# Two-block fp32 model on one core: order and diagonals of the first product and its convolution rearranged, four modulation products moved behind it

## The chip, the cores and the metric

The kernel runs on one core of one Trainium2 chip. The metric is the device time of one execution in microseconds (us). TensorE (PE) multiplies, VectorE (DVE) and ScalarE (ACT) do elementwise work, GpSimd (POOL) a little of it, and SyncE (SP) issues nearly all transfers from memory, in one queue. Each engine takes its instructions in the order in which the program issues them; they wait for each other by semaphores.

## The reference, cut to what matters

Two model blocks on a sequence of 256 positions with 1024 features, all in fp32. The change touches only the beginning of the first one:

```
c_act = silu(c)
mod = c_act @ mod_w + mod_b                  # 6 vectors of 1024: sh_m, sc_m, gt_m, sh_f, sc_f, gt_f
h = rmsnorm(x, norm_pre_mix) * (1 + sc_m) + sh_m
u = h @ a_pw1_w + a_pw1_b                    # first product: 1024 -> 2048
a, gt = split(u)
u = a * sigmoid(gt)
u = causal_dwconv(u, a_dw_w) + a_dw_b        # depthwise, 31 taps
u = silu(layernorm(u, a_ln_g, a_ln_b))
y = u @ a_pw2_w + a_pw2_b                    # second product: 1024 -> 1024
x = x + gt_m * rmsnorm(y, norm_post_mix)
h = rmsnorm(x, norm_pre_ffn) * (1 + sc_f) + sh_f
...                                          # a feed-forward part, then the second block's two layers
```

## The kernel before

Activations lie with features on the partitions: eight input tiles of 128 features x 256 positions. A fp32 product is made of three passes of a rounded format: each operand is split into a high part (rounded) and a low part (what is left). For a weight block of 128 x 1024 (a unit), ScalarE makes the high part (`split_hi`, tile `whi`) and VectorE the low part (`split_lo`, tile `wlo`, the difference). Weights come two units (1 MB) at a time into three buffers `wraw`; a buffer is loaded again as soon as the second difference of its block is done.

The modulation `c_act @ mod_w` is not a TensorE product: for each of 48 groups of 128 outputs, a block `mraw` of 128 x 1024 is loaded (five buffers), VectorE multiplies it by the broadcast row `cact` (`mod_mult`), and ScalarE sums along the row (`mod_sum`). Groups 0 to 15 give shift and scale for the eight input tiles of the first product; 16 to 39 are needed behind the second product.

`pointwise_conv` begins with warm-up products on a zero tile, the broadcast of `cact`, and the root mean square of x (statistics tile `st`, square root, reciprocal, transposes into `bc`, copy `rms`). Then comes the first product, one input tile k after the other: VectorE makes two modulation products, ScalarE two sums, VectorE scales the tile (`scaled`), adds the bias to the two modulation values (`mod`), ScalarE modulates it (`y`) and rounds it (`xh`), VectorE makes the low part (`xl`), and TensorE makes 48 products (`pw1`) into eight banks of output tiles. The banks are turned into the convolution's inputs by a sigmoid on ScalarE (`sg`) and a product on VectorE (`up`); the sigmoid's bias lies in the table `vecs`, which `load_consts` loads.

The convolution of seven output tiles runs on TensorE: a diagonal tile (`conv_stack`, on GpSimd) holds the taps, and copies of the input shifted by 0 to 3 positions (`shifts`; TensorE, then `sh` by ScalarE) are multiplied by it. The eighth tile's 31 taps run on VectorE (`conv_dve`). A background list (`bg`) of small steps, taps and modulation products for groups 16 on, is worked off by `pump` between TensorE's parts: a call takes steps until their listed costs exceed its argument. A modulation step (`half` in `mod_later`) issues the sum of one group, the load of another and the product of the next. `pointwise_out` then ends the layer norm's statistics (`finish`), normalizes in five groups of tiles, and makes the second product (`gemm_square`): four input tiles into all outputs, then a tail in which TensorE's last output tiles alternate with VectorE's bias additions (`on_tiles`). `stream.split` inside these products keeps four units ahead.

Numbers that set the order: `MOD_LATE` modulation steps are left for the second product, `PUMPS` says after which of its input tiles they are issued and at what cost, `CV` how many roundings and differences of the second product's units are issued during the convolution and before the statistics, `LOS` in which groups of the normalization, `WARM_START` the numbers of warm-up products.

Of the kernel before, what the change touches and what calls it, by code (L numbers as in the profile page):

```python
# [25 lines left out]
MOD_LATE = 3  # L26
PUMPS = {3: 3}
CV = (5, 4)
LOS = (1, 2, 3)
MEMFILL = (4, 8, 2, 2)  # L30
WARM_START = (10, 6, 3, 24)
# [219 lines left out]
class Builder:  # L251
# [377 lines left out]
    def setup(self):  # L629
        nc = self.nc  # L630
        c = self.const
        first = "first" in self.parts
        x = self.xr.rearrange("p k t -> p (k t)")
        if first:
            self.cact = self.modp.tile([P, UNIT], F32, name="cact", bufs=1)
            nc.sync.dma_start(out=self.cact[0:1, :], in_=self.dr["c"])
        for h in range(2):
            c0 = slice(h * 4 * T, (h + 1) * 4 * T)
            nc.sync.dma_start(out=x[:, c0], in_=self.dr["x"][:, c0])
        self.head = c.tile([P, HEAD + P], F32, name="head")  # L640
# [3 lines left out]
        if first:  # L644
            self.taps = self.modp.tile([P, 288], F32, name="taps", bufs=1)
        else:
            self.load_consts()
        self.inv = c.tile([P, 1], F32, name="inv")
        nc.vector.memset(self.inv, 1.0 / 1024)
        self.one1 = c.tile([P, 1], F32, name="one1")  # L650
        nc.vector.memset(self.one1, 1.0)
        self.dummy = c.tile([P, 1], F32, name="dummy")
        self.preload(AF.Silu if first else AF.Sqrt)
        self.epst = {}
        for e in (RMS_EPS, LN_EPS, 4 * LN_EPS):
            self.epst[e] = c.tile([P, 1], F32, name=f"eps{len(self.epst)}")
            nc.vector.memset(self.epst[e], e)
        if self.need_mem:
            self.memk = c.tile([P, 2, T], F32, name="memk")
            self.memv = c.tile([P, 2, T], F32, name="memv")  # L660
# [240 lines left out]
    def conv_stack(self, cp, j):  # L901
# [4 lines left out]
        self.nc.gpsimd.tensor_tensor(out=t, in0=eye.unsqueeze(1).to_broadcast([P, 32, 32]),  # L906
# [8 lines left out]
    def pointwise_conv(self, cp):  # L915
# [3 lines left out]
        warm = self.xl[:, 0, :]  # L919
# [22 lines left out]
        def add(i, j, n):  # L942
            nc.vector.tensor_tensor(out=sq[:, i:i + n, :], in0=sq[:, i:i + n, :], in1=sq[:, j:j + n, :],
                                    op=ALU.add)

        for h, ps in enumerate(rows):
            nc.vector.tensor_copy(out=self.cact[:, 512 * h:512 * h + 512], in_=ps)
            add(4 * h, 4 * h + 2, 2)
            add(4 * h, 4 * h + 1, 1)
        add(0, 4, 1)  # L950
        st, bc = (self.ps_st.tile([P, 2, T], F32, name=nm, tag=nm) for nm in ("st", "bc"))
        for h in range(2):
            nc.tensor.matmul(st[:, 0, h:h + 1], lhsT=sq[:, 0, h * P:h * P + P], rhs=self.inv, start=True,
                             stop=True, skip_group_check=True)
        keep_warm(WARM_START[2])
# [4 lines left out]
        def mult(k):  # L960
            mods[k] = [self.mod_raw.pop(0) for _ in range(2)]
            for r in mods[k]:
                self.mod_mult(r)
                yield

        def sums(k):
            for h, r in enumerate(mods.pop(k)):
                self.mod_sum(r, h * KD + k)
                yield
            if self.n_mod < 2 * KD:  # L970
                self.mod_load(2)

        mult0, sums0 = mult(0), sums(0)
        next(mult0)
# [4 lines left out]
        keep_warm(WARM_START[3])  # L979
        rms = cp.tile([P, T], F32, name="rms", tag="sg", bufs=2)  # L980
        next(sums0)
        nc.scalar.copy(out=rms, in_=bc[:, 0, :])
        next(mult0)
# [6 lines left out]
        list(sums0)  # L990
# [6 lines left out]
        order = CONV_ORDER  # L997
        npe, ndv = N_PE_CONV, KD - N_PE_CONV
        first = [j for j in order if j >= ndv]
# [20 lines left out]
        for k in range(KD):  # L1020
            y, sh, sc = self.ys[:, k, 0, :], mod[:, 0, k:k + 1], mod[:, 1, k:k + 1]
            xh, xl = self.xh[:, k, :], self.xl[:, k, :]
            if k:
                next(mults)
                self.stream.split_hi()
                self.stream.split_hi()
                list(sums(k))
                self.stream.split_lo()
# [3 lines left out]
            if k:  # L1032
                nc.scalar.activation(out=y, in_=y, func=AF.Identity, scale=sc, bias=sh)
                nc.scalar.copy(out=xh, in_=y)
            else:
# [4 lines left out]
                self.stream.split_lo()  # L1040
            if k < KD - 1:
                mults = mult(k + 1)
                if k:
                    next(mults)
            nc.vector.tensor_tensor(out=xl, in0=y, in1=xh.bitcast(F32), op=ALU.subtract)
            if k == 0:
                next(mults)
# [74 lines left out]
        for n, j in enumerate(first):  # L1122
# [10 lines left out]
            if n >= npe - CV[0]:  # L1133
# [14 lines left out]
    def pointwise_out(self, st, later):  # L1148
# [3 lines left out]
        for _ in range(CV[1]):  # L1152
            self.stream.split_lo()
        bc = st.finish(LN_EPS, AF.Silu, False)
        groups = self.apply_tiles()
# [8 lines left out]
        for i, (k0, k1) in enumerate(groups):  # L1164
# [1129 lines left out]
```

## Time and profile before

| | us |
|---|---|
| three runs | 1480.75, 1483.52, 1484.99 (median 1483.52) |
| the profiled execution, device time | 1481.87 |
| its span, from first to last instruction | 1480.1 |
| TensorE busy in the span | 1419.9 (96%) |
| VectorE busy | 1076.0 (73%) |
| ScalarE busy | 853.8 (58%) |
| first product's matrix products, first to last | 16.9 to 73.0 |
| first tap of the convolution on VectorE | 74.0 |
| second product, first to last | 128.8 to 155 |
| first product of the feed-forward part | 180.3 |

All rows below are of the profiled execution, times from its span's start. A busy share of an engine counts an instruction that has begun and waits inside for another engine's access as busy. Durations of neighbours overlap a little, so that two instructions of 1.22 in a row take 2.35.

### The profile page before, as it was taken

The numbers are of one execution on the slowest core, as the hardware profiler recorded it, in microseconds if no ns is written. First come the engines' busy times: TensorE is split into PE (matmuls) and PEld (weight loads), VectorE is DVE, ScalarE is ACT, GpSimd is POOL, SyncE is SP. The second block draws the span as 40 slices with busy tenths as digits, with TensorE's granted clock in tenths as the row PEclk, the third lists the DMA queues.
The fourth block names the chain that finished last, engine by engine and source line by source line (L and its number), as shares of the span: only waits on it lengthen the run. The fifth ranks groups of instructions, "written<-read, shape, count | busy, mean of one in ns | idle before, by whom it ended". The sixth has DMA issues, their size and how long they took to land. (4 is left out here: it accounts for less than half of the span.)

```text
span 1480.1 us, 26075 instructions
## 1 busy us (share of the span) xinstructions
PE 1419.9 (96%) x10664; PEld 1273.4 (86%) x10664; DVE 1076.0 (73%) x1705; ACT 853.8 (58%) x1505; POOL 119.6 (8%) x113
## 2 busy tenths in 40 slices
PE   8888899999999999999999999999999999999997
PEld 7867799998888888898788888888888888888886
DVE  7897788885777656788568776678766765787754
ACT  6787566684655535751346555466554676565542
POOL 1210100001000010031010000110001111100011
PEclk9998899999999999999999999999999999999998
DMA  9774445565355553240024555536554342265540
GB/s 379 292 243 186 170 155 189 198 234 207 136 202 179 196 199 136 86 143 4 2 109 167 184 196 181 189 143 221 182 195 187 136 143 86 91 226 196 196 174 29
DMA packets 39145, 250.38 MB, mean 169 GB/s; under 512 B 4337, under 2 KB 4849, under 8 KB 12274
## 3 DMA queue, kind: packets, MB, share of 16 engines
q1 hardware_dynamic: 38594, 247.60, 45.9%
q8 instruction: 84, 1.38, 0.4%
q10 hardware_dynamic: 432, 1.11, 0.2%
q14 instruction: 35, 0.29, 0.1%
HBM read 247.65 MB, written 1.05 MB: 168 GB/s over the span
## 5 line engine op out<-in xcount | busy, mean ns | idle before, releaser
L235 DVE TENSOR_TENSOR wlo<-wraw,whi 128x1024 fp32r<-128x1024 f32 x416 | 514.3, 1250 | 34.1 <-ACT whi L226 33.4
L226 ACT CAST whi<-wraw 128x1024 fp32r<-128x1024 f32 x416 | 426.3, 1045 | 22.0 <-PE acc L378 5.6
L384 PE MATMUL acc<-hx,whi 128*128 128x512 f32 x880 | 310.7, 398 | 0.0
L384 PE MATMUL acc<-xx,whi 128*128 128x512 f32 x816 | 284.1, 390 | 0.0
L372 PE MATMUL acc<-xx,wlo 128*128 128x256 f32 x1008 | 280.7, 284 | 0.0
L372 PE MATMUL gu<-xx,wlo 128*128 128x256 f32 x1008 | 279.0, 282 | 1.6 <-ACT xx L625 1.0
L372 PE MATMUL acc<-hx,wlo 128*128 128x256 f32 x880 | 247.5, 281 | 0.0
L384 PEld LDWEIGHTS acc<-hx,whi 128*128 128x128 f32 x880 | 165.3, 188 | 40.5
L372 PEld LDWEIGHTS gu<-xx,wlo 128*128 128x128 f32 x1008 | 189.9, 189 | 4.9 <-ACT xx L625 1.7
L372 PEld LDWEIGHTS acc<-xx,wlo 128*128 128x128 f32 x1008 | 190.9, 191 | 0.8
L384 PEld LDWEIGHTS acc<-xx,whi 128*128 128x128 f32 x816 | 153.2, 188 | 32.1
L372 PEld LDWEIGHTS acc<-hx,wlo 128*128 128x128 f32 x880 | 166.1, 189 | 0.0
L384 PE MATMUL gu<-xx,whi 128*128 128x512 f32 x432 | 150.9, 390 | 0.0
L377 PE MATMUL gu<-xx,whi 128*128 128x256 f32 x512 | 148.4, 290 | 2.4 <-ACT u L894 2.4
L378 PE MATMUL gu<-xx,whi 128*128 128x256 f32 x512 | 142.9, 279 | 0.0
L1331 ACT ACTIVATE ys<-ys 128x256 f32<-128x256 f32 (+1 forms) x66 | 28.6, 437 | 151.7 <-DVE ys L1249 134.9
L377 PEld LDWEIGHTS gu<-xx,whi 128*128 128x128 f32 x512 | 96.2, 188 | 10.8 <-issue 7.9
L378 PEld LDWEIGHTS gu<-xx,whi 128*128 128x128 f32 x512 | 96.3, 188 | 0.7 <-issue 0.7
L384 PEld LDWEIGHTS gu<-xx,whi 128*128 128x128 f32 x432 | 81.1, 188 | 17.0
L1348 POOL TENSOR_TENSOR nsum<-ys 128x512 f32<-128x512 f32 (+1 forms) x9 | 12.4, 1380 | 871.1 <-PE acc L384 452.3
L858 ACT COPY lows<-acc 128x256 f32<-128x256 f32 x55 | 20.6, 374 | 97.8 <-PE acc L384 97.6
L1247 DVE SCALAR_TENSOR_TENSOR ys<-xr,acc 128x256 f32<-128x256 f32 x32 | 13.5, 422 | 75.0 <-PE acc L384 75.0
(397 smaller groups left out, 2351.5 us busy)
## 6 DMA issues: line engine op xcount, KB each, us to landing
wraw<-in_w SPq DMA_DIRECT2D x208, 1024.0 KB, 4.8
mraw<-in_mod SPq DMA_DIRECT2D x48, 512.0 KB, 5.5
xr<-in_x SPq DMA_DIRECT2D x2, 512.0 KB, 4.2
m<-in_mem SPq DMA_DIRECT2D x1, 1024.0 KB, 8.2
out<-xr SPq DMA_DIRECT2D x3, 256.0 KB, 2.2
cst<-in_consts SPq DMA_DIRECT2D x1, 546.0 KB
lora<-in_lora ACTq DMA_DIRECT2D x1, 384.0 KB, 3.4
lora_g<-in_lora ACTq DMA_DIRECT2D x1, 384.0 KB, 3.9
```

Source lines behind the costliest of these rows:

```text
L226: b.nc.scalar.copy(out=hi, in_=raw)
L235: b.nc.vector.tensor_tensor(out=lo, in0=raw, in1=hi.bitcast(F32), op=ALU.subtract)
L372: self.nc.tensor.matmul(out, lhsT=wl, rhs=x[:, 0, :], start=start, stop=False, skip_group_check=True)
L377: mm(out, lhsT=wh, rhs=x[:, 0, :], start=start, stop=False, skip_group_check=True)
L378: mm(out, lhsT=wh, rhs=x[:, 1, :], start=False, stop=False, skip_group_check=True)
L384: self.nc.tensor.matmul(bank, lhsT=wh, rhs=x, start=False, stop=stop, skip_group_check=True)
L858: nc.scalar.copy(out=lows[:, 1, :], in_=banks[1][:, 1, :])
L1247: self.nc.vector.scalar_tensor_tensor(out=y, in0=self.xr[:, k, :], scalar=2 * ALPHA, in1=ps[:, 1, :], op0=ALU.mult, op1=ALU.add)
L1331: b.nc.scalar.activation(out=b.ys[:, k0:k1, 1, :], in_=y, func=AF.Square)
L1348: e.tensor_tensor(out=out[:, q:2, :], in0=prev[:, q:2, :], in1=t[:, q:2, :], op=ALU.add)
```

## The change

- The table of taps is loaded as the second transfer of all, and five diagonals are made at the beginning, three of them on VectorE and two on GpSimd. Before, it was loaded behind input tile 1 and GpSimd made all five behind tile 2. The last two diagonals stay on GpSimd in the convolution.
- The squares of x are no longer added on VectorE; TensorE sums them with sixteen products of one column. The warm-up products go from 10, 6, 3, 24 to 10, 0, 14, on a tile that input tile 7 uses last.
- The operand of an input tile has its own function, called behind the product of the tile before. Both modulation products of a tile are made at its beginning, and the second rounding copy of its weights stands behind both sums.
- `load_consts` is called behind tile 6's product instead of tile 5's.
- In the convolution's background list a modulation product follows every second tap, where one followed every tap. Seven modulation steps instead of three are left for later: one is issued before the layer norm's statistics, one, two and two behind input tiles 1, 2 and 3 of the second product, the last one behind its tail.
- Before the statistics one difference is issued instead of four, one more behind them, and then one in each of four groups instead of three.

```
-MOD_LATE = 3
-PUMPS = {3: 3}
-CV = (5, 4)
-LOS = (1, 2, 3)
+MOD_LATE = 7
+PUMPS = {1: 1.1, 2: 2.2, 3: 2.2}
+CV = 5
...
-WARM_START = (10, 6, 3, 24)
+WARM_START = (10, 0, 14)
...
             nc.sync.dma_start(out=self.cact[0:1, :], in_=self.dr["c"])
+            self.taps = self.modp.tile([P, 288], F32, name="taps", bufs=1)
+            nc.sync.dma_start(out=self.taps, in_=self.dr["taps"])
...
-        warm = self.xl[:, 0, :]
+        warm = self.xl[:, KD - 1, :]
...
+        stacks = [self.conv_stack(cp, j, nc.vector if n < 3 else None)
+                  for n, j in enumerate(first[:N_STACK])]
         for h, ps in enumerate(rows):
             nc.vector.tensor_copy(out=self.cact[:, 512 * h:512 * h + 512], in_=ps)
-            add(4 * h, 4 * h + 2, 2)
-            add(4 * h, 4 * h + 1, 1)
-        add(0, 4, 1)
...
-        for h in range(2):
-            nc.tensor.matmul(st[:, 0, h:h + 1], lhsT=sq[:, 0, h * P:h * P + P], rhs=self.inv, start=True,
-                             stop=True, skip_group_check=True)
-        keep_warm(WARM_START[2])
+        for k in range(KD):
+            for h in range(2):
+                nc.tensor.matmul(st[:, 0, h:h + 1], lhsT=sq[:, k, h * P:h * P + P], rhs=self.inv,
+                                 start=k == 0 and h == 0, stop=k == KD - 1, skip_group_check=True)
...
-        for k in range(KD):
+        def operand(k):
+
             y, sh, sc = self.ys[:, k, 0, :], mod[:, 0, k:k + 1], mod[:, 1, k:k + 1]
             xh, xl = self.xh[:, k, :], self.xl[:, k, :]
             if k:
-                next(mults)
+                mult(k)
                 self.stream.split_hi()
+                sums(k)
                 self.stream.split_hi()
-                list(sums(k))
-                self.stream.split_lo()
                 scaled(k, rms)
                 self.stream.split_lo()
...
                 nc.scalar.copy(out=xh, in_=y)
+                self.stream.split_lo()
...
+        operand(0)
+        for k in range(KD):
             pw1(k)
-            if k == 1:
-                nc.sync.dma_start(out=self.taps, in_=self.dr["taps"])
-            elif k == 2:
-                stacks = [self.conv_stack(cp, j) for j in first[:N_STACK]]
-            elif k == 5:
+            if k < KD - 1:
+                operand(k + 1)
+            if k == 6:
                 self.load_consts()
             if k > 4:
-                self.mod_load(5 - len(self.mod_raw) - (k < KD - 1))
+                self.mod_load(5 - len(self.mod_raw))
...
-            if mods:
+            if mods and i % 2:
                 self.bg.append(mods.pop(0))
...
-        for _ in range(CV[1]):
-            self.stream.split_lo()
+        self.stream.split_lo()
+        self.pump(1.0)
         bc = st.finish(LN_EPS, AF.Silu, False)
+        self.stream.split_lo()
...
-            if i in LOS:
-                self.stream.split_hi()
+            if i:
                 self.stream.split_lo()
+                if i < 4:
+                    self.stream.split_hi()
```

Three places show what moves. On VectorE, one input tile of the first product; a name's number is its buffer or version (`mraw` a modulation block, `wlo` a difference, `xx` the operand's low part). Before:

```order
L235 TENSOR_TENSOR wlo_373<-wraw_121,whi_363 128x1024
L986 SCALAR_TENSOR_TENSOR ys_78<-xr_73,head_88,rms_206 128x256
L235 TENSOR_TENSOR wlo_376<-wraw_121,whi_365 128x1024
L1031 TENSOR_TENSOR mod_135<-mod_135,sbias_216 128x2
L720 TENSOR_TENSOR mraw_214<-mraw_214,cact_84 128x1024
L1045 TENSOR_TENSOR xx_77<-ys_78,xx_77 128x256
L720 TENSOR_TENSOR mraw_297<-mraw_297,cact_84 128x1024
```

Now:

```order
L719 TENSOR_TENSOR mraw_120<-mraw_120,cact_84 128x1024
L719 TENSOR_TENSOR mraw_210<-mraw_210,cact_84 128x1024
L980 SCALAR_TENSOR_TENSOR ys_78<-xr_73,head_90,rms_208 128x256
L234 TENSOR_TENSOR wlo_374<-wraw_122,whi_363 128x1024
L1021 TENSOR_TENSOR mod_136<-mod_136,sbias_217 128x2
L234 TENSOR_TENSOR wlo_379<-wraw_122,whi_371 128x1024
L1031 TENSOR_TENSOR xx_77<-ys_78,xx_77 128x256
```

The same seven instructions; the modulation products now stand ahead of the tile's own work and the second difference behind the modulation's addition. On ScalarE, the same tile (`whi` a rounding copy, `mraw,mod` a sum). Before:

```order
L226 CAST whi_363<-wraw_121 128x1024
L226 CAST whi_365<-wraw_121 128x1024
L724 ACTIVATE mraw_119,mod_135<-mraw_119 128x1024
L724 ACTIVATE mraw_212,mod_135<-mraw_212 128x1024
L1033 ACTIVATE ys_78<-ys_78,mod_135 128x256
L1034 CAST xx_77<-ys_78 128x256
```

Now:

```order
L225 CAST whi_363<-wraw_122 128x1024
L723 ACTIVATE mraw_120,mod_136<-mraw_120 128x1024
L723 ACTIVATE mraw_210,mod_136<-mraw_210 128x1024
L225 CAST whi_371<-wraw_122 128x1024
L1023 ACTIVATE ys_78<-ys_78,mod_136 128x256
L1024 CAST xx_77<-ys_78 128x256
```

The second rounding copy went behind the two sums. On SP, the loads at the end of the first product (`in_w` weights, `in_mod` modulation blocks). Before:

```order
L733 DMA mraw<-in_mod 128x1024 x2
L204 DMA wraw<-in_w 128x2048
L663 DMA vecs<-in_vecs 128x710
L664 DMA cst<-in_consts 128x1092
L733 DMA mraw<-in_mod 128x1024
```

Now:

```order
L732 DMA mraw<-in_mod 128x1024
L203 DMA wraw<-in_w 128x2048 x2
L732 DMA mraw<-in_mod 128x1024 x3
L203 DMA wraw<-in_w 128x2048
L662 DMA vecs<-in_vecs 128x710
L663 DMA cst<-in_consts 128x1092
```

The two tables stand two weight blocks later, behind the block (the eleventh) that waits for tile 7's differences. On VectorE, from the last normalized tiles of the second product's input to the first bias additions (`ys<-acc0`). Before:

```order
L626 TENSOR_TENSOR xx_77<-ys_78,xx_77 128x2x256
L235 TENSOR_TENSOR wlo_1467<-wraw_1382,whi_1453 128x1024
L1161 TENSOR_TENSOR ys_78<-ys_78,bc_1419 128x2x256
L626 TENSOR_TENSOR xx_77<-ys_78,xx_77 128x2x256
L235 TENSOR_TENSOR wlo_1559<-wraw_1382,whi_1465 128x1024
L720 TENSOR_TENSOR mraw_1237<-mraw_1237,cact_84 128x1024
L720 TENSOR_TENSOR mraw_1250<-mraw_1250,cact_84 128x1024
L235 TENSOR_TENSOR wlo_1652<-wraw_1388,whi_1557 128x1024
L1179 TENSOR_SCALAR ys_78<-acc0_1481,vecs_90 128x256 x2
```

Now:

```order
L625 TENSOR_TENSOR xx_77<-ys_78,xx_77 128x2x256
L234 TENSOR_TENSOR wlo_1446<-wraw_732,whi_1417 128x1024
L719 TENSOR_TENSOR mraw_1176<-mraw_1176,cact_84 128x1024
L234 TENSOR_TENSOR wlo_1513<-wraw_1402,whi_1429 128x1024
L719 TENSOR_TENSOR mraw_1217<-mraw_1217,cact_84 128x1024
L719 TENSOR_TENSOR mraw_1229<-mraw_1229,cact_84 128x1024
L234 TENSOR_TENSOR wlo_1549<-wraw_1402,whi_1439 128x1024
L719 TENSOR_TENSOR mraw_1355<-mraw_1355,cact_84 128x1024
L719 TENSOR_TENSOR mraw_1510<-mraw_1510,cact_84 128x1024
L234 TENSOR_TENSOR wlo_1639<-wraw_1427,whi_1547 128x1024
L1168 TENSOR_SCALAR ys_78<-acc0_1457,vecs_92 128x256 x2
```

Behind the last low parts stand four differences and five modulation products where two and two stood.

## Rows read from the trace of the kernel before

**Rows 1.** Windows of 10 us: engines' busy time (instructions), clock, DMA share, GB/s.

```profile
20.00:30.00 10.00, 7.88 (x65) 7.48 (x64) 10.00 (x13) 7.37 (x14) 0.00 (x0) 1.00 1.02 412
...
40.00:50.00 10.00, 7.75 (x44) 7.46 (x45) 10.00 (x10) 6.29 (x11) 4.55 (x2) 0.66 0.57 198
```

**Rows 2.** Timeline of VectorE in the first product: start, us, what.

```profile
27.40 0.48 DVE L986 SCALAR_TENSOR_TENSOR ys<-xr,head,rms 128x256 f32<-128x256 f32 x1
...
32.81 2.14 DVE L986 SCALAR_TENSOR_TENSOR ys<-xr,head,rms 128x256 f32<-128x256 f32 x1
```

**Rows 3.** Timeline of GpSimd: the five diagonals.

```profile
32.41 12.15 POOL L906 TENSOR_TENSOR stack<-taps 128x1024 f32<-128x1024 f32 x5 [31.96 <-DMA taps<-in_taps]
```

**Rows 4.** Timeline of all engines at the start.

```profile
7.47 1.65 PE L925 MATMUL acc<-xx 128*128 128x256 f32 x6
...
9.93 0.98 PE L953 MATMUL st<-inv,ys 128*128 128x1 f32 x4 [0.82 <-DVE ys L943]
...
10.78 0.99 PE L925 MATMUL acc<-xx 128*128 128x256 f32 x3
...
12.63 0.48 DVE L986 SCALAR_TENSOR_TENSOR ys<-xr,head,bc 128x256 f32<-128x256 f32 x1
...
16.91 0.40 PE L1009 MATMUL gu<-xx,whi 128*128 128x256 f32 x2
```

**Rows 5.** Timeline of ScalarE in the last tiles of the first product.

```profile
60.17 2.00 ACT L226 CAST whi<-wraw 128x1024 fp32r<-128x1024 f32 x2
62.07 1.06 ACT L724 ACTIVATE mraw<-mraw 128x1024 f32<-128x1024 f32 x1
...
65.28 0.41 ACT L1034 CAST xx<-ys 128x256 fp32r<-128x256 f32 x1
```

**Rows 6.** Timelines of ScalarE and VectorE: first and last sigmoid, first tap.

```profile
68.18 0.47 ACT L1099 ACTIVATE sg<-gu,vecs 128x256 f32<-128x256 f32 x1 [0.98 <-PE gu L1009]
...
73.07 0.47 ACT L1099 ACTIVATE sg<-bc,vecs 128x256 f32<-128x256 f32 x1 [0.22 <-PE bc L1009]
73.98 0.41 DVE L1084 TENSOR_SCALAR ys<-up,vecs 128x256 f32<-128x256 f32 x1
```

**Rows 7.** SP's issue of vecs; transfers to 140 us: count, KB, us to landing.

```profile
54.32 0.42 SPq L663 DMA_DIRECT2D vecs<-in_vecs  x1
...
mraw<-in_mod SPq DMA_DIRECT2D x42, 512.0 KB, 5.6
...
m<-in_mem SPq DMA_DIRECT2D x1, 1024.0 KB, 8.2
...
vecs<-in_vecs SPq DMA_DIRECT2D x1, 355.0 KB, 8.2
```

**Rows 8.** Timelines from the convolution's end to the root.

```profile
106.46 3.49 PE L1128 MATMUL acc<-sh,stack 128*32 128x256 f32 x64
112.43 5.22 PE L1128 MATMUL acc<-sh,stack 128*32 128x256 f32 x64 [2.48 <-ACT sh L1076]
...
113.99 4.12 DVE L1088 SCALAR_TENSOR_TENSOR ys<-up,vecs,ys 128x256 f32<-128x256 f32 x8
...
120.20 4.63 DVE L235 TENSOR_TENSOR wlo<-wraw,whi 128x1024 fp32r<-128x1024 f32 x4
...
125.11 0.29 ACT L1396 ACTIVATE sd<-sd,eps 128x2 f32<-128x2 f32 x1 [2.22 <-DVE sd L1394]
```

**Rows 9.** Timelines at the end of the second product.

```profile
144.85 2.35 DVE L720 TENSOR_TENSOR mraw<-mraw,cact 128x1024 f32<-128x1024 f32 x2
...
148.26 0.87 DVE L1179 TENSOR_SCALAR ys<-acc,vecs 128x256 f32<-128x256 f32 x2
149.64 1.23 DVE L235 TENSOR_TENSOR wlo<-wraw,whi 128x1024 fp32r<-128x1024 f32 x1 [0.50 <-ACT whi L226]
...
152.10 0.38 PE L377 MATMUL acc<-xx,whi 128*128 128x256 f32 x1 [1.02 <-DVE ys L1179]
...
159.69 0.25 ACT L1398 ACTIVATE sd<-st,eps 128x2 f32<-128x2 f32 x1
```

More of the change, by code (lines that the diff above doesn't have):

```diff
@@ L643, in setup @@
         self.cst = c.tile([P, NCONST], F32, name="cst")
-        if first:
-            self.taps = self.modp.tile([P, 288], F32, name="taps", bufs=1)
-        else:
+        if not first:
             self.load_consts()
@@ L898, in conv_gate, with conv_stack @@
         nc.vector.tensor_tensor(out=hl, in0=h, in1=hh.bitcast(F32), op=ALU.subtract)
-    def conv_stack(self, cp, j):
+    def conv_stack(self, cp, j, eng=None):
         taps, eye = self.taps[:, :256].rearrange("p (j i) -> p j i", j=KD), self.taps[:, 256:]
         t = cp.tile([P, 32, 32], F32, name="stack", bufs=N_STACK)
-        self.nc.gpsimd.tensor_tensor(out=t, in0=eye.unsqueeze(1).to_broadcast([P, 32, 32]),
+        (eng or self.nc.gpsimd).tensor_tensor(out=t, in0=eye.unsqueeze(1).to_broadcast([P, 32, 32]),
                                      in1=taps[:, j, :].unsqueeze(2).to_broadcast([P, 32, 32]), op=ALU.mult)
@@ L940, in pointwise_conv @@
         self.preload(AF.Sqrt)
-        def add(i, j, n):
-            nc.vector.tensor_tensor(out=sq[:, i:i + n, :], in0=sq[:, i:i + n, :], in1=sq[:, j:j + n, :],
-                                    op=ALU.add)
+        order = CONV_ORDER
+        npe, ndv = N_PE_CONV, KD - N_PE_CONV
+        first = [j for j in order if j >= ndv]
+        stacks = [self.conv_stack(cp, j, nc.vector if n < 3 else None)
+                  for n, j in enumerate(first[:N_STACK])]
         for h, ps in enumerate(rows):
             nc.vector.tensor_copy(out=self.cact[:, 512 * h:512 * h + 512], in_=ps)
-            add(4 * h, 4 * h + 2, 2)
-            add(4 * h, 4 * h + 1, 1)
-        add(0, 4, 1)
         st, bc = (self.ps_st.tile([P, 2, T], F32, name=nm, tag=nm) for nm in ("st", "bc"))
-        for h in range(2):
-            nc.tensor.matmul(st[:, 0, h:h + 1], lhsT=sq[:, 0, h * P:h * P + P], rhs=self.inv, start=True,
-                             stop=True, skip_group_check=True)
-        keep_warm(WARM_START[2])
+        for k in range(KD):
+            for h in range(2):
+                nc.tensor.matmul(st[:, 0, h:h + 1], lhsT=sq[:, k, h * P:h * P + P], rhs=self.inv,
+                                 start=k == 0 and h == 0, stop=k == KD - 1, skip_group_check=True)
         sd = self.tmp.tile([P, 2], F32, name="sd", tag="sd")
@@ L963, in mult @@
                 self.mod_mult(r)
-                yield
         def sums(k):
@@ L968, in sums @@
                 self.mod_sum(r, h * KD + k)
[L969 to L974, printed above, removed]
+                if self.n_mod < 2 * KD:
+                    self.mod_load(1)
+        mult(0)
         nc.vector.reciprocal(out=sd, in_=sd)
@@ L978, in pointwise_conv @@
                                 identity=self.k("ident"))
-        keep_warm(WARM_START[3])
+        keep_warm(WARM_START[2])
         rms = cp.tile([P, T], F32, name="rms", tag="sg", bufs=2)
-        next(sums0)
+        sums(0)
         nc.scalar.copy(out=rms, in_=bc[:, 0, :])
-        next(mult0)
         def scaled(k, rms):
@@ L989, in pointwise_conv @@
         scaled(0, bc[:, 0, :])
-        list(sums0)
         self.mark("pw1")
@@ L996, in pointwise_conv @@
         mod = self.mod[:, :2 * KD].rearrange("p (a k) -> p a k", a=2)
-        order = CONV_ORDER
-        npe, ndv = N_PE_CONV, KD - N_PE_CONV
-        first = [j for j in order if j >= ndv]
         banks = [self.acc_tile(i) for i in range(4)] + [self.gu_tile(), self.gu_tile()] + [
@@ L1132, in pointwise_conv @@
                     self.pump(slot)
-            if n >= npe - CV[0]:
+            if n >= npe - CV:
                 self.stream.split_hi()
@@ L1151, in pointwise_out @@
         self.preload(AF.Sqrt)
-        for _ in range(CV[1]):
-            self.stream.split_lo()
+        self.stream.split_lo()
+        self.pump(1.0)
         bc = st.finish(LN_EPS, AF.Silu, False)
+        self.stream.split_lo()
         groups = self.apply_tiles()
```

5 lines of the change are left out of this document (removed).

## The prediction

> **What bounds the kernel now.** I read the stretches by windows first, then each engine in order of time, then the queue's transfers. Only the first 180 us hold changed work; behind them TensorE runs dense products, so whatever moves their start moves the end by as much.
>
> VectorE bounds the first product. From 40 to 50 it is busy 10.00 of 10 us with ten instructions, where 20 to 30 held thirteen [rows 1]: some only wait. The scaling of an input tile takes 0.48 at 27.40 and 2.14 at 32.81, 1.66 more [rows 2]; the time between these two, 5.41, is a tile's undisturbed period. GpSimd makes five diagonals in just that time, 12.15 from 32.41 [rows 3], so they cost VectorE about 5 x 1.66 = 8.3. In the convolution VectorE runs without a break up to the four differences at 120.20, and behind the second product TensorE waits 1.02 at 152.10 for VectorE's bias additions [rows 8, 9].
>
> **Start: +1.6.** The adds of the squares go from VectorE, and sixteen one-column products (32 passes) replace two (4 passes). Passes come (10.78 - 9.93)/4 = 0.2125 apart [rows 4]; from 7.47, where the six dropped warm-up products stood, they last 6.8, to 14.3, and the square root (the root, below) follows at 14.45. Both sums now stand on ScalarE before the copy of the scale, and by its waits scaling starts behind that copy (12.63 before). Root 0.15, two sums 2.1, copy 0.4, scaling 0.4, bias and the modulation's addition 0.5 put the first operand at 18.0 to 18.45 and the first product near 18.5 instead of 16.91. The three diagonals on VectorE are in no row; as a 1024-wide product of two operands, like a modulation product, and in turn with the two on GpSimd, they take 3 x 1.2 + 2 x 1.66 = 6.9. Two copies (1.3) and two modulation products (2.3) follow, so all is hidden behind the root if their table lands by 3.9. If it took the 8.2 of vecs [rows 7] from its issue near 1.2, they would cost 5.5; but the queue is empty here and the table has 144 KB, so I take nothing.
>
> **First product: -4.7 at its end.** The stall of 8.3 goes. What is late next is a loop between VectorE and ScalarE: by the order, the second rounding copy (whi) moved behind both sums. From a tile's start: two modulation products 2.35, the second one's sum 1.05 (3.4), the copy 1.0 (4.45), the second difference 1.15 (5.6), the low operand 0.35: 5.96 instead of 5.41 [rows 5, 8, 9]. No row of before has this sequence, so the bounds are 5.41, if the wait vanishes, and 5.96; I take 5.96, a sum of measured pieces. The loop's rewriting itself gains nothing: before and after, product k and operand k+1 follow each other on every engine with nothing of another tile between them, so TensorE is fed no tile earlier. Behind the first operand (0.4 + 0.4 + 0.4 and two differences) VectorE is free at 21.5; six periods and 5.4 later tile 7's high operand is ready at 62.7, against 65.28 + 0.41 = 65.7. TensorE needs 8 x (73.07 - 68.18)/7 = 5.6 for a tile, so it ends at 68.3 instead of 73.0 [rows 5, 6].
>
> **Vectors: 4.0 of that lost again.** Before, the load of vecs (the sigmoid's bias is in it) was issued at 54.32 and took 8.2: done before the first sigmoid at 68.18 [rows 6, 7]. Now it stands behind operand 7 in SP's queue, after the weight block whose buffer that tile's second difference frees at 63.0; so it is issued at 63.4. It lands 5.6 (median of the modulation loads) to 8.2 later, 69.0 to 71.6. With fewer loads queued than at 54.32 I take 69.0. Eight sigmoids 0.5 apart then put the first tap at 73.3, only 0.7 before the old 73.98; the other end is 1.9 behind it.
>
> The Trainium skill (SBUF — State Buffer, Summary: rules for kernel authors) says to estimate transfers from HBM at about 358 GB/s; this trace moved 412 in a full stretch [rows 1]. By the page the 1.4 MB of weight block and vecs would take 0.5 us longer and the sum would be 0.5 higher, an estimate; I go by the trace.
>
> **Convolution: +2.2.** From first tap to root it was 125.11 - 73.98 = 51.1. Now two taps stand together, the second waiting for the first (0.515, from 4.12 for eight [rows 8]): 0.515 + 0.4 + 1.14 = 2.05 a group. Fifteen groups 30.7, two diagonals left on GpSimd 3.4, one addition 0.6 and the tap itself 0.5 put the last tap at +35.2. Sums stand in ScalarE's queue ahead of the copies that TensorE's next tile needs, so behind it come in a row: square 0.3, sum 1.05, rounding 0.95, output and square 0.8, copies 1.0, two sums 2.1, rounding 0.95, output and square 0.8, copies 1.0, TensorE's last tile 3.5, output and square 0.9, table 1.4, the pumped sum 1.05, statistics 0.6: 16.4. That makes 51.6, 0.5 more, with the three differences that no longer precede the root already out. TensorE now idles near 4 us a tile: after 2.48 idle its last tile took 5.22 instead of 3.49: the array ran slow for part of it. One such tile on the path costs 1.7, none 0, two 3.5; I take one. So the root comes 1.5 later than 125.11. The one difference put behind the statistics takes 1.15 where VectorE waited 1.0 for TensorE: +0.2. The second product is 1.7 late.
>
> **Behind the second product: +5.2, +1.05, +1.15.** By the order VectorE has nine full-width instructions before its first bias addition at 148.26, where it had four: 2.35/2 and 4.63/4 give 1.15 each, 5.7 more. Queued behind them are the additions, and for those TensorE waits already, so nothing covers this. The last modulation block is loaded behind a weight block freed by the sixth difference and behind the 1 MB of mem. Landing 5.6 after its issue it is in time; if mem takes its old 8.2 and that block comes 1.3 behind, VectorE waits 3.1. I take the median, so 0. The wait of 0.50 for a rounding copy at 149.64 goes. One more sum stands before the root at 159.69: 1.05 [rows 7, 9]. TensorE idles about 6 us before its last 24 products; at the slow passes' rate (0.2125) they take 2.3 more. The tile at 112.43 lost half of what a wholly slow one would (1.7 of 3.5), so I take 1.15.
>
> **Sum.** 1.7 + 5.7 - 0.5 + 1.05 + 1.15 = +9.1. On the profiled execution's 1481.87 (span 1480.1) that is 1491.0. It lies 1.65 under the median of the runs, 1483.52, so I forecast 1492.6.
>
> **Rivals.**
> - VectorE's work is the only bound (faster). Then the 8.3 counts whole, less the start's 1.6, and moved modulation products are only moved: -6.7, 1476.8. For it: VectorE has no idle time through the first product [rows 1, 2]. Against it: the 0.55 per tile that the new sequence opens, and the place of vecs. It decides if the bias additions start before 149.
> - The start's gain survives (same). If vecs lands before 64.5, the first tap comes 4.7 earlier, not 0.7; with no slow tile in the convolution: +9.1 - 4.0 - 1.7 = +3.4, 1486.9. For it: the queue is emptier at 63 than at 54. Against: the load would have to land 1 us after its issue, or tile 7 be done 4 us sooner.
> - Clock and queue go against it (slower still): vecs at 8.2 (2.6), a second slow tile (1.8), the wait for mem (3.1): +16.6, 1500.1.
>
> **Chances.** 0.3% is 4.45 us, about what a measurement of this kernel can tell from no change. Forecast 0.56, slower still 0.12, gain survives 0.20, VectorE alone 0.12. So slower 0.68, same 0.20, faster 0.12. The range takes in most of the second rival and half the way to the third: 1483.5 to 1498; the likeliest case's own is 1488 to 1496.
>
> **What would show it.** Right: no stretched VectorE instruction between 30 and 50; a tile's period near 6.0 with some 0.6 idle before its second difference, released by ScalarE's whi; the first sigmoid released by the load of vecs, some 5 us behind TensorE's first finished bank; the first bias addition near 155 and TensorE idle some 6 us there, released by VectorE. Wrong: a period of 5.4, sigmoids paced by TensorE, a first tap before 71, or a wait of TensorE in the second product under 3 us.

## The result: 11.0 us slower, and the profile after

| | us |
|---|---|
| before, median of 4 runs | 1483.91 |
| after, median of 4 runs (1493.83 to 1495.83) | 1494.94 |
| ratio, 95% interval | 1.0077 (1.0065 to 1.0089) |
| the profiled execution, device time (span) | 1493.83 (1492.0) |

The forecast was 1492.6. The two profiled executions lie 12.0 apart; four marks tell where 11.5 of that arose. The *first root* is that of the layer norm's statistics, the *last root* the first one behind the second product:

| | first tap | first root | first bias addition | last root |
|---|---|---|---|---|
| before [rows 6, 8, 9] | 73.98 | 125.11 | 148.26 | 159.69 |
| after | 73.92 | 127.02 | 158.13 | 171.19 |
| difference | -0.06 | +1.91 | +9.87 | +11.50 |

From the last root to the end of the span the two take 1320.4 and 1320.9, so nearly nothing arose behind it.

The first product, timelines of all engines after (start, us, engine, line, operation; in brackets the idle time before it and what ended it). These answer to [rows 2 to 6]:

```profile
3.39 6.92 DVE L905 TENSOR_TENSOR stack<-taps 128x1024 f32<-128x1024 f32 x3 [2.12 <-DMA taps<-in_taps]
...
3.44 5.79 POOL L905 TENSOR_TENSOR stack<-taps 128x1024 f32<-128x1024 f32 x2 [3.00 <-DMA taps<-in_taps]
...
7.47 6.99 PE L952 MATMUL st<-inv,ys 128*128 128x1 f32 x32
...
18.55 0.50 PE L999 MATMUL gu<-xx,whi 128*128 128x256 f32 x2
...
29.76 0.48 DVE L980 SCALAR_TENSOR_TENSOR ys<-xr,head,rms 128x256 f32<-128x256 f32 x1
...
31.99 1.23 DVE L234 TENSOR_TENSOR wlo<-wraw,whi 128x1024 fp32r<-128x1024 f32 x1 [0.55 <-ACT whi L225]
...
35.74 0.48 DVE L980 SCALAR_TENSOR_TENSOR ys<-xr,head,rms 128x256 f32<-128x256 f32 x1
...
62.43 0.41 ACT L1024 CAST xx<-ys 128x256 fp32r<-128x256 f32 x1
...
63.55 0.43 SPq L662 DMA_DIRECT2D vecs<-in_vecs  x1
...
69.02 0.28 PE L999 MATMUL bc<-xx,wlo 128*128 128x256 f32 x1
...
69.37 0.84 ACT L1086 ACTIVATE sg<-gu,vecs 128x256 f32<-128x256 f32 x2 [5.02 <-PE bc L999]
...
73.92 0.40 DVE L1071 TENSOR_SCALAR ys<-up,vecs 128x256 f32<-128x256 f32 x1
```

The scaling takes 0.48 in every tile, the stretched 2.14 is gone, and a tile's period is 35.74 - 29.76 = 5.98. Operand 7 is ready at 62.84 instead of 65.69. Then ScalarE stands still for 5.02 before its first sigmoid. The label names TensorE's last bank, but seven banks were ready by then, and the first sigmoid reads another one; it starts 5.8 behind the issue of vecs, and the second follows without a gap. The window that answers to [rows 1] (busy time of PE, PEld, DVE, ACT, POOL, then granted clock, DMA share, GB/s) has thirteen VectorE instructions again, in 8.89:

```profile
40.00:50.00 10.00, 10.00 (x88) 10.00 (x87) 8.89 (x13) 8.40 (x14) 0.00 (x0) 1.00 1.00 368
```

The convolution's end, TensorE and ScalarE, and then two windows; against [rows 8]:

```profile
94.18 3.37 PE L1059 MATMUL gu<-up,head 128*32 128x256 f32 x32 [4.90 <-ACT sh L1063]
...
97.85 1.06 ACT L723 ACTIVATE mraw<-mraw 128x1024 f32<-128x1024 f32 x1 [0.90 <-DVE mraw L719]
99.90 1.06 ACT L723 ACTIVATE mraw<-mraw 128x1024 f32<-128x1024 f32 x1 [0.91 <-DVE mraw L719]
...
114.97 8.06 PE L1115 MATMUL acc<-sh,stack 128*32 128x256 f32 x128
...
127.02 0.29 ACT L1385 ACTIVATE sd<-sd,eps 128x2 f32<-128x2 f32 x1 [0.41 <-DVE sd L1383]
```

```profile
94.00:104.00 10.00, 7.30 (x108) 4.13 (x112) 9.82 (x16) 8.03 (x16) 0.00 (x0) 0.84 0.78 258
104.00:114.00 10.00, 7.41 (x111) 4.68 (x107) 9.82 (x14) 7.87 (x15) 0.00 (x0) 0.83 0.67 211
```

TensorE waits for ScalarE's copies (4.90 here), and two of the sums that stand ahead of the next copies wait 0.90 each for VectorE.

The end of the second product, against [rows 9]:

```profile
147.36 0.37 SPq L756 DMA_DIRECT2D m<-in_mem  x1
147.82 3.98 SPq L732 DMA_DIRECT2D mraw<-in_mod  x3
...
152.46 1.22 DVE L719 TENSOR_TENSOR mraw<-mraw,cact 128x1024 f32<-128x1024 f32 x1
155.86 1.22 DVE L719 TENSOR_TENSOR mraw<-mraw,cact 128x1024 f32<-128x1024 f32 x1 [2.18 <-ACT whi L225]
157.00 1.22 DVE L234 TENSOR_TENSOR wlo<-wraw,whi 128x1024 fp32r<-128x1024 f32 x1
158.13 0.87 DVE L1168 TENSOR_SCALAR ys<-acc,vecs 128x256 f32<-128x256 f32 x2
...
161.37 0.58 PE L376 MATMUL acc<-xx,whi 128*128 128x256 f32 x1 [7.33 <-DVE ys L1168]
...
171.19 0.25 ACT L1387 ACTIVATE sd<-st,eps 128x2 f32<-128x2 f32 x1
```

TensorE's wait for VectorE's additions grew from 1.02 to 7.33. Ahead of them VectorE itself waits 2.18 before the last modulation product, whose block was queued behind the 1 MB of `mem` (the second block's memory input, multiplied right behind the second product). The label names ScalarE; e3 and e8 below show that it is the block.

### The profile page after: what moved, and what is told of

Its sections match the earlier page's. It is cut to its first block, busy times and chain, and to the rows that moved or that the text cites. A ratio compares the mean times of both kernels' runs of the same rounds, so it can differ in the third digit from the quotient of the medians.

```text
span 1492.0 us, 26077 instructions
## 1 busy us (share of the span) xinstructions
PE 1426.2 (96%) x10673; PEld 1277.7 (86%) x10673; DVE 1072.3 (72%) x1703; ACT 854.3 (57%) x1505; POOL 112.4 (8%) x110
## 3 DMA queue, kind: packets, MB, share of 16 engines
HBM read 247.65 MB, written 1.05 MB: 167 GB/s over the span
```

## The experiments

Times are medians against the kernel before, measured anew with each (1482.5 to 1484.5). The ratios, as recorded, differ from those of the medians by up to 0.001, which is 1.5 us. The marks are of one profiled execution each. From its last root to the end these took 1320 to 1326, though nothing is changed there, so marks and medians can differ by some us. "After" is the changed kernel, "before" the kernel before.

| run | us to before | ratio, 95% interval | first tap | first root | bias addition | last root |
|---|---|---|---|---|---|---|
| after | +11.0 | 1.0077 (1.0065, 1.0089) | 73.92 | 127.02 | 158.13 | 171.19 |
| e1_tables_early | +6.7 | 1.0046 (1.0034, 1.0058) | 70.31 | 123.25 | 154.01 | 167.07 |
| e2_tail_old | +2.6 | 1.0021 (1.0012, 1.0029) | 74.00 | 124.63 | 150.11 | 163.07 |
| e3_mem_behind | +11.0 | 1.0083 (1.0070, 1.0096) | 74.19 | 128.46 | 157.32 | 170.97 |
| e4_diag_alone | -3.7 | 0.9983 (0.9971, 0.9994) | 71.47 | 122.86 | 146.13 | 157.44 |
| e5_first_part | -1.3 | 0.9997 (0.9987, 1.0007) | 74.23 | 125.07 | 148.22 | 159.65 |
| e6_first_part_tables | -4.7 | 0.9975 (0.9963, 0.9986) | 70.29 | 122.52 | 145.67 | 157.11 |
| e7_rounding_first | -7.7 | 0.9958 (0.9942, 0.9973) | 68.91 | 119.43 | 142.58 | 154.02 |
| e8_warm_tail | +10.0 | 1.0073 (1.0058, 1.0088) | 74.20 | 127.28 | 158.14 | 169.71 |
| e9_every_tap | +6.0 | 1.0038 (1.0024, 1.0053) | 73.88 | 120.99 | 151.83 | 164.78 |
| e10_sums_first | -8.4 | 0.9946 (0.9933, 0.9959) | 66.84 | 117.29 | 140.43 | 151.85 |
| e11_four_in_gaps | -9.3 | 0.9931 (0.9914, 0.9948) | 66.83 | 114.07 | 137.82 | 149.25 |
| e12_four_between | -6.2 | 0.9950 (0.9933, 0.9967) | 66.79 | 113.81 | 141.49 | 152.82 |

**The late tables.**

```
-            if k == 6:
+            if k == 4:
                 self.load_consts()
```

> The changed kernel with the load of the two tables (vecs, constants) called behind input tile 4's product instead of tile 6's. The changed kernel stands 11.0 us above the kernel before. Theory (the late table takes the first product's whole gain): the sigmoids now follow TensorE bank by bank, the first near 64.4 instead of 69.4, the first tap near 70.1 instead of 73.9, and all that follows comes 3.8 earlier: 7.2 above the kernel before. Rival 1 (the convolution's end hangs on TensorE, ScalarE and the weights, not on the first tap): the first tap comes early, the layer norm's root stays near 127: still 11.0 above. Rival 2 (the tables' 0.9 MB delay the modulation blocks of the first product): tiles take longer than 6.0 each, the gain is under 2: more than 9 above.

First and last sigmoid on ScalarE in this run:

```profile
64.50 0.48 ACT L1086 ACTIVATE sg<-gu,vecs 128x256 f32<-128x256 f32 x1
...
69.41 0.47 ACT L1086 ACTIVATE sg<-bc,vecs 128x256 f32<-128x256 f32 x1 [0.22 <-PE bc L999]
```

The wait of 5.02 is gone, the sigmoids are paced by TensorE (0.22 each), and first tap, first root and last root come 3.6, 3.8 and 4.1 earlier. The theory holds; the 4.4 in the medians is all of it and not absorbed.

**The second half undone, in two steps.** First only the modulation products:

```
-MOD_LATE = 7
-PUMPS = {1: 1.1, 2: 2.2, 3: 2.2}
+MOD_LATE = 3
+PUMPS = {3: 3}
...
-            if mods and i % 2:
+            if mods:
...
-        self.pump(1.0)
         bc = st.finish(LN_EPS, AF.Silu, False)
```

> The changed kernel with the modulation products put back to where the kernel before has them: one after every tap, three steps left for the second product and issued behind its input tile 3 only, none ahead of the statistics. The four differences behind the low parts stay as changed. Theory (the four products moved there are the largest part of the loss): behind the low parts VectorE has two modulation products less three (-3.4), no wait for the last modulation block (-2.2), one sum less before the last root (-1.05), the slow clock of the last products shorter (-1), no sum ahead of the first root (-1.05); the convolution takes up to 4.2 more by ScalarE's four more sums, of which I take 1.5: together -7, that is 4 above the kernel before. Rival (the work is only displaced: the four products and sums cost the convolution as much as they cost the tail, 4.6 or more): -3.5 or less, at least 7.5 above.

It came 8.4 below after, a little more than the theory's 7; "only displaced" falls. The price of 1.5 for four more sums in the convolution was wrong in sign: the first root is 2.4 earlier although four products and sums came back into it (e9_every_tap below tells why). Next the differences too, as before:

```
-        self.stream.split_lo()
+        for _ in range(4):
+            self.stream.split_lo()
         bc = st.finish(LN_EPS, AF.Silu, False)
-        self.stream.split_lo()
...
-            if i:
+            if i in (1, 2, 3):
+                self.stream.split_hi()
                 self.stream.split_lo()
-                if i < 4:
-                    self.stream.split_hi()
```

> The changed kernel with the second half of the change undone: background list, differences and modulation products of the convolution, the statistics and the second product as in the kernel before. Start, diagonals, the order of the operands and the late tables stay as changed. Theory (the first half of the change nets to nothing, since the late tables take back what the diagonals gave; all of the 11.0 lies behind the first tap): first tap near 73.9, first root near 125.1, the end as in the kernel before, 0 within 1. Rival (the first half itself costs something, by the convolution's slower clock): 2 to 4 above the kernel before.

No difference from before can be measured, at the marks neither. So the first half of the change nets to nothing, and the place of the differences costs 163.07 - 159.65 = 3.4 at the last root. From first root to bias addition it is 25.48 in e2_tail_old and 23.15 here: the two extra differences behind the low parts, 2.3. Three fewer ahead of the root gave 0.4 of that back. The other 1.5 arose behind the bias addition. In e2_tail_old TensorE waits 2.76 there (1.08 in e5_first_part), and its last 24 products stand 0.213 apart instead of 0.117, the low level of its clock (granted clock 0.52 from 154 to 160, here 1.00):

```profile
153.67 0.58 PE L376 MATMUL acc<-xx,whi 128*128 128x256 f32 x1 [2.76 <-DVE ys L1167]
```

```profile
154.00:160.00 6.00, 6.00 (x31) 6.00 (x31) 3.19 (x7) 2.50 (x6) 2.80 (x3) 0.52 1.02 420
```

That the slow products make up this 1.5 is argued from the rows; e8_warm_tail below tests it in after.

**The diagonals alone**, on the kernel before:

```
...
+        stacks = [self.conv_stack(cp, j, nc.vector if n < 3 else None)
+                  for n, j in enumerate(first[:N_STACK])]
         def add(i, j, n):
...
-                stacks = [self.conv_stack(cp, j) for j in first[:N_STACK]]
```

> The kernel before with one part of the change alone: the table of taps loaded second, and the five diagonals made at the start, three on VectorE and two on GpSimd. Order of the operands, squares, tables, convolution and second product stay as before. Theory (the diagonals beside VectorE cost the first product 8.3, and this is a true loss): the start comes 2 later (VectorE's copies and adds of squares wait until 10.3), a tile's period is 5.4 throughout, the last sigmoid comes 5 to 6 earlier, and all behind it as well: 5.5 below the kernel before. Rival 1 (only VectorE's order is relieved and TensorE or the weights' loads bound the first product): 0 to 2 below. Rival 2 (the first tap comes early, but the convolution's end hangs on other engines): the root of the layer norm stays near 125, no change in the end.

Faster, by 3.7 where 5.5 was expected: between theory and rival 1. Two rows from its first product:

```profile
28.82 0.84 PE L1012 MATMUL gu<-xx,whi 128*128 128x256 f32 x2 [2.04 <-ACT xx L1037]
```

```profile
30.00:34.00 4.00, 4.00 (x24) 4.00 (x23) 4.00 (x6) 3.59 (x7) 0.00 (x0) 0.57 1.03 368
```

The diagonals hold VectorE until 10.2, its adds of the squares come behind them, and the first product starts at 20.9, 4.0 later than in [rows 4]. Then TensorE waits 2.04 once, runs at 0.57 of its clock for the next 4 us, and is the bound itself from there. The stall of 8.3 was real, but TensorE had only part of it to give: with a start 4.0 later it ends the first product 2.5 earlier. This profiled execution, at 1485.3, is the slowest of its twelve: it is 2.3 ahead at the last root and loses 5.7 behind it, so the 3.7 stands on the medians.

**Tables and rounding order on top of the first half.** First e5_first_part with the edit of e1_tables_early:

> As e5_first_part, with the tables' load called behind input tile 4's product. Theory: the first tap comes at 70.2 instead of 73.9 and everything with it, 3.8 below e5_first_part and so 3.8 below the kernel before. Rival (the convolution, with VectorE's old load in it, absorbs the earlier first tap): less than 1.5 below e5_first_part.

Measured 3.4 below e5_first_part (first tap 3.9, first root 2.6 earlier): the theory, with a remainder lost in the convolution. Next:

```
                 mult(k)
                 self.stream.split_hi()
+                self.stream.split_hi()
                 sums(k)
-                self.stream.split_hi()
```

> As e6_first_part_tables, with both rounding copies of a tile's weights ahead of the two sums again. VectorE's wait of 0.55 before the second difference should go, a tile's period fall from 5.98 to 5.65. Theory (from tile 1 on TensorE needs 5.64 a tile, so it becomes the bound): the first product ends 1.1 earlier, first tap near 69.1, 4.9 below the kernel before. Rival 1 (VectorE's period counts whole): 7 x 0.33 = 2.3 earlier, 6.1 below. Rival 2 (ScalarE's loop keeps the period at 6.0): as e6_first_part_tables, 3.8 below.

VectorE's scalings in this run:

```profile
23.78 0.48 DVE L980 SCALAR_TENSOR_TENSOR ys<-xr,head,rms 128x256 f32<-128x256 f32 x1
29.18 0.48 DVE L980 SCALAR_TENSOR_TENSOR ys<-xr,head,rms 128x256 f32<-128x256 f32 x1
```

The period falls to 5.40, yet the first tap comes only 1.4 earlier: TensorE is the bound, as the theory has it. The 3.0 in the medians is more than that, but the two intervals overlap; from first tap to first root this execution took 50.5 and e6_first_part_tables 52.2, and why is not settled.

**The wait for the last modulation block.**

```
-        self.nc.sync.dma_start(out=m.rearrange("p k t -> p (k t)"), in_=self.dr["mem"])
+        self.bg.insert(1, (0.0, lambda: self.nc.sync.dma_start(
+            out=m.rearrange("p k t -> p (k t)"), in_=self.dr["mem"])))
```

> The changed kernel with the 1 MB load of mem queued behind the load of the last modulation block instead of ahead of it; nothing else moves. Theory (VectorE's wait of 2.18 at 155.86 is this block, late because mem lies ahead of it in the queue): the wait goes, the first bias addition comes near 156.0 instead of 158.1, TensorE's idle time ahead of the last products falls from 7.3 to about 5, and the end comes 2.2 to 2.7 earlier: 8.5 above the kernel before. Rival (the wait is for ScalarE's rounding copy, as the profile labels it, or the block is late by the weight block queued ahead of both): the wait stays, 11.0 above.

VectorE and TensorE there:

```profile
153.91 2.35 DVE L719 TENSOR_TENSOR mraw<-mraw,cact 128x1024 f32<-128x1024 f32 x2
156.18 1.22 DVE L234 TENSOR_TENSOR wlo<-wraw,whi 128x1024 fp32r<-128x1024 f32 x1
157.32 0.87 DVE L1169 TENSOR_SCALAR ys<-acc,vecs 128x256 f32<-128x256 f32 x2
...
160.55 0.58 PE L376 MATMUL acc<-xx,whi 128*128 128x256 f32 x1 [5.07 <-DVE ys L1169]
```

The mechanism is right: the wait is gone, and from first root to bias addition it takes 28.86 instead of 31.11. The end does not show it. This execution's convolution took 1.2 longer, and from bias addition to last root it took 0.6 longer, TensorE's last 24 products still 0.213 apart. What the wait is worth at the end stays open.

**The slow clock of the last products.**

```
+        self.warm = 60
         self.gemm_square(st, on_tiles)
...
+        if getattr(self, "warm", 0):
+            self.keep_warm(self.warm)
+            self.warm = 0
         ws = [self.stream.take(False) for _ in range(2)]
```

> The changed kernel with 60 products that nobody reads (60 x 0.117 = 7.0) on TensorE in its idle time of 7.3 ahead of the last 24 products of the second product. Theory (those 24 ran at the low clock, 0.2125 apart instead of 0.117, because TensorE had idled, and this is a term of its own of 2.3): clock 1.00 from 154 to 166, the last root 2.3 earlier, 8.7 above the kernel before. Rival (VectorE's additions and ScalarE's squares pace the tail, or the products fed in delay it): last root not earlier, 11.0 above or more.

Timelines of VectorE and TensorE, then windows:

```profile
155.86 1.23 DVE L722 TENSOR_TENSOR mraw<-mraw,cact 128x1024 f32<-128x1024 f32 x1 [1.90 <-DMA mraw<-in_mod]
...
161.37 0.38 PE L376 MATMUL acc<-xx,whi 128*128 128x256 f32 x1 [0.61 <-DVE ys L1171]
```

```profile
156.00:162.00 6.00, 5.39 (x46) 5.19 (x45) 6.00 (x9) 3.24 (x5) 1.25 (x2) 1.00 1.02 415
162.00:168.00 6.00, 4.50 (x34) 3.98 (x33) 4.39 (x9) 4.66 (x10) 1.78 (x2) 1.00 0.64 237
```

The clock stays at 1.00 (0.71 and 0.72 in the same windows of after), the 24 products take 3.0 instead of 4.7, and the last root comes 1.5 earlier: less than 2.3, since 18 of the 24 had been slow. Then the products of `mem` run partly at the low level (0.72 from 168 to 174, as in after). At the end the intervals of both kernels overlap, so a gain there is not shown. Here the row names what the wait of VectorE is for: the load of the modulation block.

**Paired taps.**

```
-            if mods and i % 2:
+            if mods:
```

> The changed kernel with a modulation product after every tap in the convolution instead of after every second one; all else, the seven steps left for later too, as changed. In the changed kernel first tap to root takes 53.1, with the products and sums put back as well (e2_tail_old) 50.6. Theory (pairing the taps holds the modulation's sums back, so that they stand in ScalarE's queue ahead of the copies for the last output tiles): the root comes 1.3 earlier than 127.0 and the end with it, 9.7 above the kernel before; the rest of e2_tail_old's 2.4 is the sum ahead of the statistics. Rival (only the sum and the difference ahead of the statistics make the root late): root at 127.0, 11.0 above.

Theory and rival both fall: the first root comes 6.0 earlier, and the end 5.0. ScalarE's sums, answering to those at 97.85 and 99.90 of after, one of TensorE's waits for the copies, and the windows:

```profile
97.83 1.07 ACT L723 ACTIVATE mraw<-mraw 128x1024 f32<-128x1024 f32 x1
98.89 1.05 ACT L723 ACTIVATE mraw<-mraw 128x1024 f32<-128x1024 f32 x1
99.93 1.05 ACT L723 ACTIVATE mraw<-mraw 128x1024 f32<-128x1024 f32 x1
...
120.99 0.29 ACT L1385 ACTIVATE sd<-sd,eps 128x2 f32<-128x2 f32 x1 [0.41 <-DVE sd L1383]
```

```profile
97.51 1.98 PE L1059 MATMUL gu<-up,head 128*32 128x256 f32 x32 [1.83 <-ACT sh L1063]
```

```profile
94.00:104.00 10.00, 6.93 (x132) 4.89 (x123) 9.26 (x14) 9.23 (x17) 0.00 (x0) 1.00 0.91 293
104.00:114.00 10.00, 8.76 (x160) 7.00 (x160) 9.61 (x18) 6.33 (x13) 0.00 (x0) 1.00 0.61 210
```

With a product after every tap VectorE runs ahead of ScalarE, and the sums stand back to back, 1.05 apart. Paired, a sum that has caught up waits for two taps and a product, 2.05 apart; the copies that TensorE needs are queued behind those sums, and TensorE, which waits 4.90, 2.51 and 2.59 for them in after and 1.21, 1.83 and 2.40 here, also runs partly at the low level there (0.84 and 0.83 against 1.00).

**Towards a faster kernel.** On e7_rounding_first, `mult(0)` and `sums(0)` go ahead of the first square root:

> As e7_rounding_first, with the first tile's two sums issued on ScalarE ahead of the root mean square's square root instead of behind it. ScalarE waits 4.35 there for TensorE's sixteen one-column products (32 passes), and the two sums (2.1) then stand between the root and the first operand. Theory: the sums fill that wait, the first product starts at 17.5 instead of 18.55 and everything comes 1.0 earlier: 8.7 below the kernel before. Rival (ScalarE's four rounding copies of the first weights or TensorE's slow second tile take it back): 7.7 below, as e7_rounding_first.

TensorE there:

```profile
15.82 3.33 PE L924 MATMUL acc<-xx 128*128 128x256 f32 x14
18.95 0.63 PE L999 MATMUL gu<-xx,whi 128*128 128x256 f32 x2
26.07 0.84 PE L999 MATMUL gu<-xx,whi 128*128 128x256 f32 x2 [0.41 <-ACT xx L1024]
```

```profile
26.00:34.00 8.00, 7.85 (x65) 7.65 (x66) 8.00 (x11) 7.59 (x12) 0.00 (x0) 1.00 1.00 392
```

The first tap comes 2.1 earlier (1.0 expected), the end 0.7 in the medians, whose intervals overlap. The theory's mechanism fails: the first product starts at 18.95, 0.4 later and not 1.0 earlier, because the 14 warm-up products stand ahead of it in TensorE's queue. VectorE does run 0.5 earlier (the second tile is scaled at 23.26 instead of 23.78), and the gain comes at the second tile: TensorE, later done with the first, waits 0.41 for it instead of 2.09, starts it 0.5 earlier (26.07 for 26.59) and runs the next 8 us at 1.00, where e7_rounding_first shows 0.79. No expectation held this; that the first tap gained more than the 1.0 is luck. Then the deferral that the change wanted, seven steps late (`MOD_LATE = 7`), four of them in the normalization's groups. In e11:

```
-        self.bg = later
+        self.bg = later[4:]
...
+            if i:
+                self.mod_sum(self.mod_raw.pop(0), 40 - MOD_LATE + i - 1)
+                self.mod_load(1)
             norm(i, 1)
...
             norm(i + 1, 0)
+            if i:
+                self.mod_mult(self.mod_raw[0])
```

> As e10_sums_first, with four modulation steps taken out of the convolution as the change does (a product still after every tap), but put into the normalization's groups 1 to 4: the sum on ScalarE ahead of a group's addition, where ScalarE waits 1.28 to 1.54 for VectorE, the product on VectorE ahead of a group's low part, where it waits 1.2 to 1.8 for ScalarE. Theory (deferring four products is worth about 4 at the first root, as e9_every_tap showed, and costs nothing if they stand where their engine waits): first root 4 earlier than in e10_sums_first, first bias addition too, 12.4 below the kernel before. Rival (in the groups they lengthen the loop of VectorE and ScalarE, 1 each): first bias addition at the same place, 8.4 below.

In e12 only `self.pump(1.0)` at the end of groups 1 to 4:

> As e11_four_in_gaps, with the four steps at the groups' ends, product and sum one behind the other, where no wait of VectorE covers the product. Theory (four products of 1.15 on VectorE's chain from the root to the bias additions): 4.6 lost of the 4 won, about 8 below the kernel before. Rival (TensorE, busy all through these groups, is what the additions wait for, and VectorE's place does not matter): 12.4 below, like e11_four_in_gaps.

Both win at the first root, 3.2 in e11 and 3.5 in e12. From there to the bias addition e12 loses 4.5, more than it won, as the theory says; e11 loses 0.6 and keeps 2.6. VectorE in e11's first such group:

```profile
119.08 1.22 DVE L719 TENSOR_TENSOR mraw<-mraw,cact 128x1024 f32<-128x1024 f32 x1
120.22 0.42 DVE L625 TENSOR_TENSOR xx<-ys,xx 128x256 fp32r<-128x256 f32 x1
```

The product stands where the low part had waited for ScalarE (0.51 here and 1.21 in the next group of e10_sums_first). All five times of e11 lie below all five of e12. e11_four_in_gaps, at 1473.19, has the lowest median here, 0.9931 (0.9914 to 0.9948) of before; its interval overlaps that of e10_sums_first, so that its lead over that kernel rests on the marks (2.6 at the last root).

## Why the forecast was right, point by point

By the runs, undone one after the other, the loss at the last root is 6.4 for the paired taps (after less e9_every_tap), 1.7 for the deferral itself (e9_every_tap less e2_tail_old), 3.4 for the differences (e2_tail_old less e5_first_part), and 0.0 for the first half: 11.5. In the medians the same steps are 5.0, 3.4, 3.9 and -1.3: the pairing is the largest part and the first half no loss either way, and the sizes are known to within about 2 us. Another order of undoing could share them out otherwise.

- **Start, +1.6:** right (18.55 for 18.5; 32 passes in 6.99 for 6.8; three diagonals 6.92 for 6.9).
- **First product, -4.7 at its end:** the period of 5.96 was right (5.98). TensorE ended at 69.3, not 68.3; this does not count, since vecs gated what follows. As a bound the loop was overrated: in e7_rounding_first tile 7 is scaled 3.5 earlier than in e6_first_part_tables (56.24 for 59.73), and TensorE's end moves by only 1.4, because behind its wait for the second operand and the slow stretch after it TensorE has no idle time left.
- **Vectors:** right. Issued at 63.55 (63.4), read 5.8 later. The first tap at 73.92 for 73.3 leaves none of the gain. The Trainium skill (SBUF — State Buffer, Summary: rules for kernel authors) gives about 358 GB/s to plan with. The stretch 60 to 70, in which vecs travelled, moved 413 here; the 5.8 lies between the 5.6 taken from the trace and the 6.1 by the page, an estimate.
- **Convolution, +2.2:** from first tap to first root 53.10, so +1.97. The size was right by luck, its story was not. I made it of a chain 0.5 longer and one slow tile; in truth it is two large effects: with the pairing alone undone this stretch takes 47.1, 4.0 less than before's 51.1, and the pairing puts 6.0 on top. A sum along one chain gave the right end without seeing that the pairing made that chain.
- **Behind the second product:** from first root to bias addition +7.96, where I had 0.2 + 5.7. The step that failed is the wait for the last modulation block: taken at 0 by the median landing, with 3.1 as the other end, it is 2.18, since `mem` lay ahead of it in the queue: `mem` landed 7.1 after its issue, and the block 7.9 after its own, not 5.6. Without this term the stretch comes to 5.8, against the 5.9 of the forecast.
- **From bias addition to last root:** -0.5 + 1.05 + 1.15 = +1.7; measured +1.63. The slow clock was 1.7 instead of 1.15, so the other two together gave about -0.1 instead of +0.55; no run separates them.
- **Rivals:** "VectorE alone" needed bias additions before 149; they came at 158. "The start's gain survives" needed vecs by 64.5 and no slow tile in the convolution. In e1_tables_early the first was met and worth 4.4, and the kernel still stood 6.7 above before: the second was not met (0.68 from 90 to 100), nor was the wait for `mem` in its sum. Of "clock and queue" the wait for `mem` came, and slow stretches in three tiles instead of one (the 32 products of the shifted copies took 3.37, 3.14 and 2.46 instead of 1.98), but inside the size forecast for the convolution. The end, 1494.9 for 1492.6, is late by about that one wait.

## What to carry to other kernels

An item that is moved off a busy stretch is paid for where it lands: the same four products cost 4.5 at a group's end and 0.6 in the gaps of their engines. When two engines alternate on a shared list, let the producer run ahead; with its products held back to every second step, the consumer's sums stood 2.05 apart instead of 1.05, in front of copies that a third engine needed. A load queued two weight blocks later can take back the gain of a whole stretch, if a buffer that comes free late stands ahead of it in the queue.

## What was not expected of the hardware

- A wait of some 2 us cost TensorE its clock at one place and not at another. In after, e4_diag_alone and e7_rounding_first it waited 2.42, 2.04 and 2.09 for the second operand, and the next stretch ran partly at the low level (0.86 and 0.72 from 26 to 34; 0.57 from 30 to 34; 0.79 from 26 to 34); in the kernel before a wait of 2.05 between 22 and 26 left the next 8 us at 1.00.
- The low level ended within one run of products: in after the first 18 of the last 24 came 0.213 apart, the others 0.117, with no idle time between. In e2_tail_old all 24 came 0.213 apart.
